# Low parts of eleven mixer weight tiles: an adding transfer onto negative high parts in place of VectorE's subtraction

## The chip, the cores and the metric

One core of one Trainium2 chip runs the whole program. The metric is device microseconds of one execution; lower is better. All tensors that cross the boundary are 32-bit floats.

## The reference, cut to what matters

The program is two transformer blocks, each of depth 2, over 512 tokens of width 1024. The change touches the second block alone, in its mixer stage, which runs once per layer (so twice):

```python
for l in range(DEPTH):                       # DEPTH = 2
    h = rmsnorm_2(x, norm_mix_g[l]) * (1.0 + sc1) + sh1
    u = h @ w_in[l]                          # 1024 -> 20 tiles of 128 columns, and 4 forget columns
    fq, fk, fv, ff, pu, rq, rk, rv, rg, cu = jnp.split(u, bounds, axis=-1)
    y_fox  = fox_attention(fq, fk, fv, ff, fox_fb[l])
    y_pool = pool_mixer(pu, pool_w[l], pool_scale[l])
    y_ret  = retention(rq, rk, rv, rg, positions, ret_gn_g[l])
    y_conv = conformer_conv(cu, conv_w[l], conv_b[l], conv_ln_g[l], conv_ln_b[l])
    mix = jnp.concatenate([y_fox, y_pool, y_ret, y_conv], axis=-1)
    x = x + g1 * (mix @ w_out[l])
    ...                                      # then the feed-forward stage
```

`conformer_conv` contains a causal convolution of 31 taps per channel over 256 channels.

## The kernel before, in words

TensorE multiplies in a fast 32-bit format (fp32r) that keeps fewer bits than a float. To keep the precision, every operand `x` is held as two tiles: a high part `hi` (the value rounded to fp32r, written by ScalarE, ACT) and a low part `lo = x - hi` (written by VectorE, DVE). A product is then three matmuls, `hi*hi`, `hi*lo` and `lo*hi` (`mm3`, lines 289 to 291: two with the weight's high part and one with its low part).

Weights are streamed. `weight_plan` (line 338) lists every weight tile in the order of use; for the mixers these are, per layer, twenty tiles of `w_in2` of 1024 x 128 values (on the chip 128 partitions x 1024 values, 512 KB), numbered t = 0 to 19, with the small tile `w_ff` ahead of t = 11, and then eight tiles of `w_out2`. Four of the twenty (`QB2`: 5, 8, 11 and 14) are scaled by 0.125 while they are split. Three steps bring a tile in:

- `load` (line 106) issues the transfer from HBM into a raw tile `wraw` on SyncE's queue (SP, line 118). There are four raw buffers; a load waits until the last reader of the tile four places back is done.
- `cut_tile` (line 184) splits it. It takes a pair `whi`, `wlo` from a pool with **two** buffers each, so the pair of tile t can only be written when TensorE has finished tile t - 2. ACT writes `whi` (line 203, or 206 for the scaled tiles), and DVE writes `wlo` (line 204, or 207).
- `next` (line 217) hands the pair to a product; it splits two tiles ahead.

In the mixers, `Mix.dense` (line 1689) multiplies one weight tile with the 512 tokens: 8 times `mm3` into a PSUM tile `dps`, of which there are two. What evacuates `dps` depends on the tile: t = 0 to 3 feed the convolution's gate, t = 4 to 6, 7 to 9, 11 to 13 and 14 to 16 are the query, key and value of four head pairs (for the first two pairs with a rotation, `roped`, lines 1767 to 1772), t = 10 and 17 feed the pooling mixer, 18 and 19 a gate.

Beside that runs the convolution, on DVE alone: `taps` (lines 2094 to 2103) issues 31 multiply-adds of 128 x 512 values for each of two channel halves, spread over the steps of the products. The scheduler is told to place each of them behind the latest weight split (`K.W.last`, lines 214 and 2098). Between the products stand the retention's and the forgetting attention's matmuls (lines 1956, 1987, 1837 and others).

The order of each engine's queue is settled when the program is built: a scheduler orders the instructions of each engine by its own model of their lengths, and on the chip every queue runs in that order. POOL (GpSimd) has little to do in the mixers: a few clears of small buffers (lines 274, 2045, 1830 and 2106) and some sums.

Of the kernel before, what the change touches and what calls it, by code (L numbers as in the profile page):

```python
# [13 lines left out]
AF = mybir.ActivationFunctionType  # L14
OP = mybir.AluOpType
# [36 lines left out]
QB1 = (9, 13, 17, 21, 26, 28, 31, 33)  # L52
QB2 = (5, 8, 11, 14)


def parts(x, bits):

    out = []
    for _ in range(3):
        e = math.floor(math.log2(abs(x)))  # L60
        c = math.floor(x / 2.0 ** (e - bits + 1)) * 2.0 ** (e - bits + 1)
        out.append(c)
        x -= c
    return out + [x]
# [6 lines left out]
def fr(ap):  # L71
    return ap.bitcast(F32)


class Weights:
# [5 lines left out]
    def __init__(self, K, raw, split, plan, bufs):  # L81
        self.K, self.tc, self.nc, self.raw, self.split, self.bufs = K, K.tc, K.nc, raw, split, bufs
        self.loads, self.cuts, self.sums = [], [], []
        for e in plan:
            n = len(self.loads)
            if e[0] == "S":
                self.loads += [(x, e[2] * 256) for x in e[1]]
                at = len(self.cuts)
                self.sums += [(at + i, f, n + m, e[2]) for i, f, m in
                              ((-4, self.sums12, 0), (-2, self.sums12, 2), (-1, self.sums34, 0), (0, self.sums34, 2))]  # L90
                self.cuts += [("S", i, n, e[2]) for i in range(7)]
            else:
                self.loads.append((e[0], e[1] * e[2]))
                self.cuts.append(("T", n, e[1], e[2], (e + (None,))[3]))
        self.tiles, self.freed, self.ready, self.by_pool = {}, set(), [], set()
        self.slots = {False: [], True: []}
        self.n_load = self.n_split = self.n_ring = 0
        self.st = {}
        self.extra = self.xraw = None
        self.depth = 2  # L100
# [80 lines left out]
                self.cut_tile(self.n_split, *c[1:])  # L181
            self.n_split += 1

    def cut_tile(self, at, n, kc, m, scale):
        self.load(n + 1)
        t = self.tiles[n]
        hi, lo = self.parts()
        if scale is None:
            pool = at in self.by_pool
            E = self.nc.gpsimd if pool else self.nc.vector  # L190
            step = kc * m // (PCH if pool else 1)
            if m < 64:

                w, hl = t[:, :kc * m].rearrange("p (k m) -> p k m", m=m), hi[:, :2 * kc * m]
                hl = hl.rearrange("p (k m) -> p k m", m=2 * m)
                self.nc.scalar.activation(hl[:, :, :m], w, AF.Copy)
                self.nc.vector.tensor_tensor(hl[:, :, m:], w, fr(hl[:, :, :m]), op=OP.subtract)
                self.ready.append((at, hl, None))
                self.free(n)
                return  # L200
            for o in range(0, kc * m, step):
                q = slice(o, o + step)
                s = self.nc.scalar.activation(hi[:, q], t[:, q], AF.Copy)  # L203
                v = E.tensor_tensor(lo[:, q], t[:, q], fr(hi[:, q]), op=OP.subtract)  # L204
        else:
            s = self.nc.scalar.activation(hi[:, :kc * m], t[:, :kc * m], AF.Copy, scale=scale)
            v = self.nc.vector.scalar_tensor_tensor(lo[:, :kc * m], t[:, :kc * m], scale, fr(hi[:, :kc * m]),
                                                op0=OP.mult, op1=OP.subtract)
        self.ready.append((at, hi[:, :kc * m].rearrange("p (k m) -> p k m", m=m),
                           lo[:, :kc * m].rearrange("p (k m) -> p k m", m=m)))  # L210
        if v.ins.engine == mybir.EngineType.DVE:
            self.last = s.ins, v.ins
        self.free(n)
# [68 lines left out]
class Kern:  # L282
# [54 lines left out]
    def weight_plan(self):  # L337
        a = self.a
        plan = []
        for l in range(2):  # L340
            for t in range(36):
                plan.append((a["w_in"][l, t], 8, 128, 0.125 if t in QB1 else None))
            for t in range(8):
                for p in range(2):
                    plan.append((a["w_out"][l, t, p], 6, 128))
        for l in range(2):
            for t in range(20):
                if t == 11:
                    plan.append((a["w_ff"][l], 8, 4))
                plan.append((a["w_in2"][l, t], 8, 128, 0.125 if t in QB2 else None))  # L350
            for t in range(8):
                plan.append((a["w_out2"][l, t], 8, 128))
            for f0, f1 in FGROUPS:
                f = f0
                while f < f1:
                    if f < FPLAIN:
                        plan += [(a["ffn_w1"][l, f], 8, 128), (a["ffn_w3"][l, f], 8, 128)]
                        f += 1
                    else:
                        plan.append(("S", [a[w][l, f + i] for w in ("ffn_w1", "ffn_w3") for i in range(2)], 4))  # L360
                        f += 2
                for t in range(8):
                    plan.append((a["ffn_w2"][l, t][:, f0 * 128:f1 * 128], f1 - f0, 128))
        return plan
# [2050 lines left out]
```

## Time and profile before

| | |
|---|---|
| three runs, us | 2479.31, 2479.59, 2483.43 (median 2479.59) |
| the profiled execution, us | 2483.87 |
| its span on the engines, us | 2482.1 |
| TensorE busy, share of the span | 95% |
| VectorE busy | 77% |
| ScalarE busy | 53% |
| GpSimd busy | 5% |
| mean granted clock of TensorE | 0.983 |

The profiled execution is 4.3 us above the median of the runs; 1.8 us of it lie outside the span. Matmuls are pipelined, so their busy times overlap: an idle TensorE is read from the gaps ahead of matmuls, not from the busy share. The products with the mixers' input weights run from 1286 to about 1440 us of the span in the first layer, and from 1892 to about 2050 us in the second.

### The profile page before, as it was taken

To read this page: it belongs to the slowest core of one execution; us is meant where nothing else is said; L and a number is where in the kernel's file an instruction comes from. 1 tells how busy PE (TensorE), PEld (TensorE's weight loads), DVE (VectorE), ACT (ScalarE), POOL (GpSimd) and SP (SyncE) were. 2 spreads that over 40 slices of the span, in tenths; PEclk is the share of its full clock that TensorE was granted. 3 is DMA by queue.
4 is the path that set the end of the run, shared out by engine and by line. 5 is a ranking of instruction groups with operands and counts; after the bars stand their busy time and mean duration, and the time that the engine had idled before them with its cause. 6 is when DMAs were issued, how large, how long until landed. Compare 5 with 4: busy or idle time off the path is not lost. (4 is left out here: it accounts for less than half of the span.)

```text
span 2482.1 us, 37640 instructions
## 1 busy us (share of the span) xinstructions
PE 2354.0 (95%) x14392; PEld 2028.6 (82%) x14392; DVE 1902.7 (77%) x3337; ACT 1326.0 (53%) x2595; POOL 113.0 (5%) x138
## 2 busy tenths in 40 slices
PE   7899999999999999999998899999999799999998
PEld 3788888888887788888786678989898578899997
DVE  5778777888457888798669868989767985967674
ACT  3566555667345665568644455535354455545453
POOL 0100000000011100000010101000001010100000
PEclk9999999999999999999999999999999999999999
DMA  6112333223422136641432122675432212242422
GB/s 257 51 50 92 96 105 100 85 88 100 153 81 76 45 124 204 211 131 50 135 99 67 58 63 86 215 242 208 141 102 74 69 57 68 85 137 69 136 65 72
DMA packets 87749, 269.67 MB, mean 109 GB/s; under 512 B 12049, under 2 KB 22545, under 8 KB 87185
## 3 DMA queue, kind: packets, MB, share of 16 engines
q1 hardware_dynamic: 78240, 232.79, 29.1%
q10 hardware_dynamic: 6912, 25.17, 2.9%
q0 software_dynamic: 2416, 9.31, 1.0%
q8 instruction: 113, 1.85, 0.3%
q14 instruction: 68, 0.55, 0.1%
HBM read 255.82 MB, written 11.40 MB: 108 GB/s over the span
## 5 line engine op out<-in xcount | busy, mean ns | idle before, releaser
L289 PE MATMUL dps<-hx,whi 128*128 128x512 f32 (+1 forms) x1040 | 412.7, 398 | 22.1 <-ACT q L1744 8.1
L291 PE MATMUL dps<-hx,wlo 128*128 128x512 f32 (+1 forms) x1040 | 400.1, 386 | 8.3 <-DVE wlo L204 4.3
L290 PE MATMUL dps<-hx,whi 128*128 128x512 f32 (+1 forms) x1040 | 401.0, 387 | 5.7 <-DVE hx L523 4.4
L203 ACT ACTIVATE whi<-wraw 128x1024 fp32r<-128x1024 f32 (+2 forms) x202 | 194.1, 964 | 272.6 <-issue 93.6
L204 DVE TENSOR_TENSOR wlo<-wraw,whi 128x1024 fp32r<-128x1024 f32 (+1 forms) x182 | 209.3, 1151 | 75.9 <-ACT whi L203 74.5
L289 PEld LDWEIGHTS dps<-hx,whi 128*128 128x128 f32 x1040 | 200.9, 193 | 51.3 <-ACT q L1744 8.9
L291 PEld LDWEIGHTS dps<-hx,wlo 128*128 128x128 f32 x1040 | 200.2, 193 | 44.5 <-DVE wlo L204 5.2
L290 PEld LDWEIGHTS dps<-hx,whi 128*128 128x128 f32 x1040 | 200.5, 193 | 31.5 <-DVE hx L523 7.1
L1162 ACT ACTIVATE ph<-PT 128x512 fp32r<-128x512 f32 (+1 forms) x280 | 152.8, 559 | 136.1 <-PE PT L1157 132.8
L1163 DVE TENSOR_TENSOR pl<-PT,ph 128x512 fp32r<-128x512 f32 (+1 forms) x280 | 175.2, 641 | 43.4 <-ACT ph L1162 41.2
L161 ACT ACTIVATE whi<-wraw 128x512 fp32r<-128x512 f32 x200 | 118.7, 625 | 102.5 <-PE spt L1520 38.4
L1145 PE MATMUL Y<-ph,vt 128*128 128x256 f32 (+1 forms) x592 | 161.8, 283 | 6.7 <-ACT ph L1162 2.8
L1157 PE MATMUL PT<-ident,P 128*128 128x128 f32 x1024 | 160.5, 276 | 5.8 <-DVE pl L1163 4.0
L1146 PE MATMUL Y<-pl,vt 128*128 128x256 f32 (+1 forms) x592 | 163.1, 291 | 2.4 <-DVE pl L1163 2.2
L290 PE MATMUL w2p<-g,whi 128*128 128x512 f32 (+1 forms) x364 | 140.9, 387 | 1.0 <-DVE g L299 1.0
L289 PE MATMUL w2p<-g,whi 128*128 128x512 f32 (+1 forms) x364 | 140.8, 387 | 0.0
L291 PE MATMUL w2p<-g,wlo 128*128 128x512 f32 (+1 forms) x364 | 140.6, 387 | 0.0
L1157 PEld LDWEIGHTS PT<-ident,P 128*128 128x128 f32 x1024 | 119.0, 141 | 23.1 <-DVE pl L1163 9.8
L1145 PEld LDWEIGHTS Y<-ph,vt 128*128 128x128 f32 x592 | 112.2, 190 | 28.5 <-ACT ph L1162 19.5
L1096 PE MATMUL S<-kt,qt 128*128 128x256 f32 (+2 forms) x576 | 127.3, 329 | 1.6 <-DVE nm L1114 0.9
L1146 PEld LDWEIGHTS Y<-pl,vt 128*128 128x128 f32 x592 | 112.3, 190 | 13.5 <-DVE pl L1163 6.0
L1115 ACT ACTIVATE P<-P,nm 128x512 f32<-128x512 f32 (+1 forms) x128 | 94.9, 742 | 47.7 <-DVE nm L1114 46.1
(474 smaller groups left out, 6387.6 us busy)
## 6 DMA issues: line engine op xcount, KB each, us to landing
wraw<-ffn_w SPq DMA_DIRECT2D x120, 512.0 KB, 4.4
wraw<-w_in SPq DMA_DIRECT2D x112, 512.0 KB, 3.5
adaw<-ada_wt SPq DMA_DIRECT2D x80, 512.0 KB, 4.0
adab<-ada_wt ACTq DMA_DIRECT2D x48, 512.0 KB, 5.1
wraw<-w_out SPq DMA_DIRECT2D x32, 384.0 KB, 3.1
aw<-ada_w SPq DMA_DIRECT2D x16, 512.0 KB, 10.2
wraw<-w_out SPq DMA_DIRECT2D x16, 512.0 KB, 3.5
bias<-bias_b SPq DMA_DIRECT2D x16, 384.0 KB, 3.7
```

The costliest lines, as they stand in the source:

```text
L161: self.nc.scalar.activation(hi[:, j * w:j * w + w], x, AF.Copy)
L203: s = self.nc.scalar.activation(hi[:, q], t[:, q], AF.Copy)
L204: v = E.tensor_tensor(lo[:, q], t[:, q], fr(hi[:, q]), op=OP.subtract)
L289: mm(ps, hi, xh, start=start, stop=False)
L290: mm(ps, hi, xl, start=False, stop=False)
L291: self.mm_last = mm(ps, lo, xh, start=False, stop=stop).ins
L1096: mm(S[:, so:so + n], Q[:, j, qc], Kt[:, i, ko:ko + n], start=i == 0, stop=i == 1)
L1145: mm(o, v, ph[:, co:co + w], start=b == 0 and n == 0, stop=False, skip_group_check=True)
L1146: mm(o, v, pl[:, co:co + w], start=False, stop=b == len(banks) - 1 and n == len(items) - 1, skip_group_check=True)
L1157: nc.tensor.transpose(pst[:, col:col + 128], ps[t][:, pc:pc + 128], K.ident)
L1162: A.activation(ph[:, :col], pst[:, :col], AF.Copy)
L1163: V.tensor_tensor(pl[:, :col], pst[:, :col], fr(ph[:, :col]), op=OP.subtract)
```

## The change

For eleven of the twenty tiles (t = 2, 3, 4, 6, 7, 9, 10, 12, 13, 15, 16), in both layers, the low part is made otherwise. ACT writes the negative of the rounded value into `wlo`; a transfer issued on POOL's queue then reads the same weight tile from HBM a second time and adds it onto `wlo` in place, which leaves `x - hi`; ACT writes `whi` as before. VectorE does nothing for these tiles. `K.W.last`, behind which the taps are placed, is not set by them.

```diff
+DMAT = (2, 3, 4, 6, 7, 9, 10, 12, 13, 15, 16)
...
-    def cut_tile(self, at, n, kc, m, scale):
+    def cut_tile(self, at, n, kc, m, scale, by_dma):
         self.load(n + 1)
         t = self.tiles[n]
         hi, lo = self.parts()
+        if by_dma:
+            w = kc * m
+            self.nc.scalar.activation(lo[:, :w], t[:, :w], AF.Copy, scale=-1.0)
+            self.nc.gpsimd.dma_start(lo[:, :w], self.loads[n][0], accum_op=OP.add)
+            self.nc.scalar.activation(hi[:, :w], t[:, :w], AF.Copy)
+            self.ready.append((at, *(x[:, :w].rearrange("p (k m) -> p k m", m=m) for x in (hi, lo))))
+            self.free(n)
+            return
         if scale is None:
...
-                plan.append((a["w_in2"][l, t], 8, 128, 0.125 if t in QB2 else None))
+                plan.append((a["w_in2"][l, t], 8, 128, 0.125 if t in QB2 else None, t in DMAT))
```

What the scheduler makes of it is seen in the queues. Lines of the changed kernel are 11 higher than those of the kernel before in everything below `cut_tile`.

ACT's queue at the start of the first layer's mixers, before (lines 203 and 206 write `whi`, 2086 evacuates a gate, 503 is part of a rotation, with half-tiles `t`):

```order
L203 ACTIVATE whi<-wraw 128x1024 x2
L2086 ACT_TABLE_LOAD
L2086 ACTIVATE th<-dps 128x512
L203 ACTIVATE whi<-wraw 128x1024
L2086 ACTIVATE th<-dps 128x512
L206 ACTIVATE whi<-wraw 128x1024
L203 ACTIVATE whi<-wraw 128x1024
L503 ACTIVATE t_13844<-dps 32x512 x3
```

The same stretch in the changed kernel (line 195 writes `whi`, 193 the negative into `wlo`, 217 a scaled `whi`):

```order
L195 ACTIVATE whi<-wraw 128x1024
L193 ACTIVATE wlo<-wraw 128x1024
L195 ACTIVATE whi<-wraw 128x1024
L2097 ACT_TABLE_LOAD
L2097 ACTIVATE th<-dps 128x512
L193 ACTIVATE wlo<-wraw 128x1024
L195 ACTIVATE whi<-wraw 128x1024
L2097 ACTIVATE th<-dps 128x512
L193 ACTIVATE wlo<-wraw 128x1024
L217 ACTIVATE whi<-wraw 128x1024
L195 ACTIVATE whi<-wraw 128x1024
L193 ACTIVATE wlo<-wraw 128x1024
```

The scheduler has put `whi` ahead of `wlo`, so the transfer of a tile starts two ACT instructions after its buffers come free, and for t = 3 and 4 a table load or an evacuation `th` stands between the two.

DVE's queue at the same place, before (204 and 207 are the subtractions, 2107 the gated input, 2100 and 2102 the taps):

```order
L204 TENSOR_TENSOR wlo<-wraw,whi 128x1024
L1842 CAST ck<-ones 64x512
L204 TENSOR_TENSOR wlo<-wraw,whi 128x1024
L2107 SCALAR_TENSOR_TENSOR hp_13599<-th,dps 128x512
L2100 TENSOR_SCALAR cacc_13601<-hp_13599,cw,v_13590 128x512
L2102 SCALAR_TENSOR_TENSOR cacc_13601<-hp_13599,cw,cacc_13601 128x512
L204 TENSOR_TENSOR wlo<-wraw,whi 128x1024
L2102 SCALAR_TENSOR_TENSOR cacc_13601<-hp_13599,cw,cacc_13601 128x512 x3
L2107 SCALAR_TENSOR_TENSOR hp_13600<-th,dps 128x512
L207 SCALAR_TENSOR_TENSOR wlo<-wraw,whi 128x1024
```

And in the changed kernel:

```order
L1853 CAST ck<-ones 64x512
L2118 SCALAR_TENSOR_TENSOR hp_13599<-th,dps 128x512
L2111 TENSOR_SCALAR cacc_13601<-hp_13599,cw,v_13590 128x512
L2113 SCALAR_TENSOR_TENSOR cacc_13601<-hp_13599,cw,cacc_13601 128x512 x4
L2118 SCALAR_TENSOR_TENSOR hp_13600<-th,dps 128x512
L218 SCALAR_TENSOR_TENSOR wlo<-wraw,whi 128x1024
```

The subtractions of t = 2, 3 and 4 are gone; the taps and the scaled tile's subtraction (t = 5) close up.

POOL's queue in the first layer's mixers, in the changed kernel (line 194 is the adding transfer; the kernel before has the same rows without it):

```order
L2117 MEMSET hp_13600 128x32
L194 DMA wlo<-w_in 128x1024 x7
L2056 MEMSET pb_14180 128x16
L2056 MEMSET pb_14181 128x16
L2056 MEMSET pb_14182 128x16
L194 DMA wlo<-w_in 128x1024 x2
L1841 MEMSET lf 128x512
L194 DMA wlo<-w_in 128x1024
L2142 TENSOR_TENSOR both<-cacc_13601,cacc_13602 128x512
L2025 TENSOR_TENSOR rst<-rst,nhalf 128x8
L194 DMA wlo<-w_in 128x1024
```

The eleven transfers stand in the order of the tiles; seven of them have nothing else of POOL's between them.

## Rows read from the trace of the kernel before

**Rows 1.** The page's first part: busy time, share of the span, instructions.
```profile
PE 2354.0 (95%) x14392; PEld 2028.6 (82%) x14392; DVE 1902.7 (77%) x3337; ACT 1326.0 (53%) x2595; POOL 113.0 (5%) x138
```

**Rows 2.** Busy time by stretch of the mixers: length, engines, granted clock, DMA share, GB/s.
```profile
1286.00:1304.00 18.00, 18.00 (x82) 14.61 (x81) 13.27 (x19) 6.38 (x7) 0.00 (x0) 1.00 0.42 140
1304.00:1346.00 42.00, 37.83 (x160) 29.48 (x159) 40.19 (x59) 21.74 (x35) 0.34 (x3) 0.96 0.17 51
1346.00:1398.00 52.00, 41.84 (x189) 30.20 (x187) 48.05 (x99) 20.43 (x34) 3.07 (x3) 0.97 0.24 78
1952.00:2004.00 52.00, 42.37 (x177) 31.06 (x175) 47.51 (x98) 20.37 (x35) 1.61 (x2) 0.90 0.24 77
```

**Rows 3.** Whom TensorE waited for, 1284 to 1412 us: total us, times, longest.
```profile
PE dps L289 <- ACT q L1744: 4.1, 2, 3.8
PE dps L289 <- DVE t L1767: 3.4, 2, 2.8
PE dps L291 <- DVE wlo L207: 2.0, 1, 2.0
PE yr L1987 <- ACT ph L298: 1.5, 1, 1.5
PE pm L289 <- ACT ph L298: 1.2, 1, 1.2
PE dps L289 <- ACT ft L1785: 0.8, 1, 0.8
...
PE cumps L1837 <- DVE lf L1832: 0.5, 1, 0.5
PE tps L1757 <- DVE ret L1993: 0.4, 1, 0.4
```

**Rows 4.** The same view in the second layer, 1890 to 2020 us.
```profile
PE dps L289 <- DVE t L1767: 3.1, 2, 2.8
```

**Rows 5.** DVE's groups by form, 1286 to 1398 us: count, busy, mean ns, idle before.
```profile
L2102 DVE SCALAR_TENSOR_TENSOR cacc<-hp,cw,cacc 128x512 f32<-128x512 f32 x60 | 43.4, 746 | 0.3
L204 DVE TENSOR_TENSOR wlo<-wraw,whi 128x1024 fp32r<-128x1024 f32 x10 | 12.2, 1215 | 2.4 <-ACT whi L203 2.4
```

**Rows 6.** ACT's timeline, 1283 to 1298 us: start, length, instruction, idle before and releaser.
```profile
1283.83 1.06 ACT L203 ACTIVATE whi<-wraw 128x1024 fp32r<-128x1024 f32 x1 [0.65 <-POOL ql L274]
1286.55 1.06 ACT L203 ACTIVATE whi<-wraw 128x1024 fp32r<-128x1024 f32 x1 [1.66 <-PE dps L290]
1287.63 1.28 ACT L2086 ACT_TABLE_LOAD   x1
1288.92 0.60 ACT L2086 ACTIVATE th<-dps 128x512 f32<-128x512 f32 x1
1291.97 1.06 ACT L203 ACTIVATE whi<-wraw 128x1024 fp32r<-128x1024 f32 x1 [2.45 <-PE dps L290]
1297.57 1.06 ACT L206 ACTIVATE whi<-wraw 128x1024 fp32r<-128x1024 f32 x1 [4.05 <-PE dps L290]
```

**Rows 7.** TensorE's timeline: the first matmuls of tile t = 2.
```profile
1286.41 0.39 PE L289 MATMUL dps<-hx,whi 128*128 128x512 f32 x1
1286.64 0.40 PE L290 MATMUL dps<-hx,whi 128*128 128x512 f32 x1
```

**Rows 8.** DMA issues: count, KB each, median us from issue to landing.
```profile
wraw<-w_in SPq DMA_DIRECT2D x112, 512.0 KB, 3.5
us<-T POOLq DMA_DIRECT2D x11, 384.0 KB, 2.6
x<-xt SPq DMA_DIRECT2D x1, 2048.0 KB, 8.2
```

**Rows 9.** POOL's transfers of line 1212: their instruction, ns min/median/max, first and last start.
```profile
L1212 POOL DMA_DIRECT2D us<-T x22: 539/542/731, 137.9 to 1179.7; - x22
```

**Rows 10.** Stretches right behind TensorE's two longest gaps; columns as in rows 2.
```profile
1332.00:1336.00 4.00, 4.00 (x12) 3.15 (x11) 3.91 (x7) 2.73 (x5) 0.14 (x2) 0.57 0.00 0
1376.00:1380.00 4.00, 2.92 (x6) 1.57 (x7) 3.97 (x12) 0.56 (x1) 0.00 (x0) 0.62 0.36 131
```

More of the change, by code (lines that the diff above doesn't have):

```diff
@@ L93, in __init__ @@
                 self.loads.append((e[0], e[1] * e[2]))
-                self.cuts.append(("T", n, e[1], e[2], (e + (None,))[3]))
+                self.cuts.append(("T", n, e[1], e[2], *(e[3:] + (None, False)[len(e) - 3:])))
         self.tiles, self.freed, self.ready, self.by_pool = {}, set(), [], set()
```

## The prediction

> **What bounds the kernel now.** I read the shares first, then the mixers by stretch, then TensorE's waits there. Over the span TensorE is busy for 95% [rows 1]; that is a mean over stages, and the change lives in two stretches of some 115 us. The view by stretch [rows 2] splits them. From 1286 to 1304 us TensorE has no gap (18.00 of 18.00) and DVE is busy for 13.27. From 1304 to 1346 it is the other way round: DVE is busy for 40.19 of 42, TensorE for 37.83. From 1346 to 1398 DVE has 48.05 of 52, TensorE 41.84. The second layer repeats this (42.37 and 47.51). So the first tiles are bound by TensorE and everything up to the end of the convolution's taps by DVE.
>
> The waits [rows 3] say what that costs. The lines shown sum to 13.9 us, four smaller ones left out. Nearly all lead back to DVE: a PSUM tile that the rotation has not yet emptied (3.4), a low part that comes late (2.0), and evacuations in which ACT and DVE take turns (4.1, 1.5, 1.2). The second layer's list is within 0.6 us of this one [rows 4].
>
> A gap has a second price. After the gaps of 2.8 and 3.8 us the granted clock of 4 us is 0.57 and 0.62 [rows 10], that is mostly the lower of the two levels (1.2 GHz), so about 4 x 0.43 = 1.7 us of full-speed work is lost behind each. After the wait of 2.0 us no such stretch shows in the first layer.
>
> **What is removed.** Eleven subtractions per layer; ten of them are in rows 5 with 1.215 us each, so 11 x 1.215 = 13.4 us of DVE per layer. In the stretches where DVE leads that takes its 88.24 of 94 us [rows 2] to about 79, and the taps (60 of them, 43.4 us [rows 5]) run earlier because nothing stands between them. I take it that the waits on DVE's backlog go: of the 4.1 all but 0.7, the whole of 3.4, 2.0, 0.5 and 0.4, and half of 1.5, 1.2 and 0.8 [rows 3]. That is 11.4; since such chains never close fully I count 11.0. With the two long gaps their clock losses go, 3.4. Removed per layer: **14.4 us**. This is DVE's whole saving seen on TensorE's path, a generous reading; the third rival takes a mean one.
>
> **What is added.** (a) ACT: eleven more passes of 1.06 us [rows 6], 11.7 us per layer on an engine that is busy for 48.55 of 112 us there [rows 2]. They lengthen evacuations that stand behind them; 1 us per layer. (b) POOL: eleven issues; one takes 0.54 us [rows 9] on an engine with 3.4 us of work in 112 [rows 2]. Behind a waiting transfer stand only clears of small buffers, a sum and a power, wanted later: nothing. Their cover is POOL's idleness; without it each would cost its 0.54. (c) SP: raw tiles are released after two ACT passes (2.12 us) instead of one and a subtraction (2.28): nothing. (d) The **new wait**: TensorE now waits for a transfer where it waited for DVE.
>
> The price of (d) hangs on one length that the trace does not show, L, from the issue of the adding transfer to TensorE's release. The nearest rows [rows 8]: a plain load of this size lands in 3.5 us; a load of 2048 KB in 8.2, so each further 512 KB costs (8.2 - 3.5) / 3 = 1.57 us; a store of 384 KB from POOL's queue lands in 2.6, so that queue by itself is not slower. Below 3.5 I see no reason for L to fall. An adding transfer must read its destination too: 3.5 + 1.57 = 5.1. And the raw tile's release starts the next raw load at the same moment: another 0 to 1.57. So 5.1 to 6.6, and I take the middle, **5.9**; the ends for the range are 3.5 and 8.2 (2048 KB: both reads, the write and the raw load, all in line).
>
> The Trainium skill, "Collectives: The Full Stack", section on the bandwidth ceiling, says that an add inside a transfer costs no cycles of its own but needs two source reads on one ring, which halves its rate; "DMA: Bandwidth & Descriptors", section on issuing engines, says that transfers of different issuing engines share the same 16 engines. By the first alone L would be 5.1 and the sum below minus 9 us; by both, 6.6 and plus 6. No row before shows an adding transfer.
>
> Now the tiles. TensorE needs 5.6 us for one (1291.97 to 1297.57, each the release of a buffer [rows 6]) and 0.23 per matmul [rows 7].
> - t = 2: `whi` starts at 1283.83, `wlo` is written by 1285.95 [rows 6]; TensorE starts the tile at 1286.41 [rows 7] and has four matmuls without a low part, to 1287.33. It waits L - 1.4.
> - t = 4: the buffers come free at the end of t = 2; then 1.06 + 0.60 + 1.06 = 2.7 [rows 6] and L, against one tile and two matmuls, 6.06. It waits L - 3.3.
> - t = 6: the same without the 0.60: L - 3.9. t = 9: four transposes on TensorE lie between: about L - 4.6.
> - t = 3, 7, 10: the second of two neighbours starts its chain while the first waits; the first's wait covers it. Nothing.
> - t = 12, 13, 15, 16: attention matmuls lie between the tiles (TensorE 41.84 of 52 [rows 2]); nothing at 5.9, something above 7.
>
> Sum of the waits: 4L - 13.2, at 5.9 **10.4 us** per layer. Those of t = 2 (4.5) and t = 4 (2.6) are near or above the gaps that lost the clock: 3.4.
>
> **The sum.** Per layer 10.4 + 3.4 + 1.0 - 14.4 = +0.4 us, for two layers about +1. Against the profiled execution 2483.87 that gives 2485; it stands 4.3 us above the median, so the median becomes **2481**: no change, out of two large terms that cancel. Runs of this kernel can tell 0.2%, 5 us, from nothing.
>
> **The rivals.**
> 1. *The adding transfer is little longer than a load*, L = 3.5 to 5.1. At 3.5 only t = 2 waits (2.1, under the gaps that cost the clock) and t = 4 (0.2): 2.3 + 1 - 14.4 = -11 per layer, -22. At 5.1: 7.2 + 1.7 + 1 - 14.4 = -4.5, -9. In the middle 2464. For it: POOL's short stores [rows 8]. Against: the second read.
> 2. *TensorE's wait on the transfer becomes the bound of the dense tiles* (slower). L = 8.2: four waits of 19.6, four clock losses of 1.7, 1 of ACT: 27.4 - 14.4 = +13 per layer, +26, so 2506. It turns slower by over 0.2% at L = 6.4. For it: three streams of 512 KB meet (DMA share 0.42 already from 1286 to 1304 [rows 2]). Against: that share falls to 0.17 to 0.24 afterwards.
> 3. *DVE's relief does not reach TensorE*: only the waits named for DVE go (3.4 + 2.0) and one clock loss, 7.1; the turns of ACT and DVE stay, ACT being fuller. At 5.9: 14.8 - 7.1 = +7.7 per layer, +15, so 2495.
>
> **How the numbers follow.** The forecast, L from 5.1 to 6.6, gives 2471 to 2486 (-9 to +6): chance 0.42, of which 0.12 lie beyond 0.2% on the fast side, 0.20 within, 0.10 on the slow side. Rival 1: 0.26. Rival 2: 0.20. Rival 3: 0.12. Faster 0.12 + 0.26 = 0.38, same 0.20, slower 0.10 + 0.20 + 0.12 = 0.42. The range reaches from the fast end of rival 1, short of its last microseconds, to just past rival 2: 2460 to 2508.
>
> **What would show it.** The transfers of line 194 landing in 5 to 6.6 us. TensorE's waits in 1286 to 1346 us: a line `dps L302 <- DMA wlo` with about four waits, the first near 4.5 us; the waits on `t` (line 1778 there) and on the scaled `wlo` gone. DVE busy for some 79 of those 94 us. Granted clock below 1 right after t = 2, where it is 1.00 now. The forecast is wrong if the waits on the transfer sum to under 5 or over 16 us per layer, or if TensorE's waits on ACT and DVE stay above 8.

## The result and the profile after

The changed kernel takes 2510.19 us (median of 6 runs, 2505.11 to 2513.12) against 2481.11 for the kernel before, run beside it (6 runs, 2479.31 to 2483.68). The ratio is 1.0116, with a 95% interval of 1.0100 to 1.0132: slower by 29 us. The forecast was 2481 with a range that ended at 2508, so the time lies just outside, on the slow side. The profiled execution has a span of 2508.6 us.

The page shows where the work went. TensorE has the same 14392 matmuls and is busy for 10 us more than in [rows 1], because some of them ran at a lower clock; VectorE (DVE) has 22 instructions fewer, ScalarE (ACT) 22 more. The second fence holds the queue of the adding transfers and their issues.

```profile
PE 2363.9 (94%) x14392; PEld 2034.8 (81%) x14392; DVE 1879.1 (75%) x3315; ACT 1345.9 (54%) x2617; POOL 131.9 (5%) x160
```

The same page's parts on DMA: queue, kind, packets, MB, share of 16 engines; then the issues, with KB each and median us to landing.

```profile
q0 software_dynamic: 5584, 20.84, 3.5%
...
wlo<-w_in POOLq DMA_DIRECT2D x22, 512.0 KB, 6.7
```

The answer for line 194, the transfer itself, gives the spread of that length:

```profile
L194 POOL DMA_DIRECT2D wlo<-w_in x22: 842/855/935, 1284.5 to 2035.6; - x22
...
DMA to landing us min/median/max: 5.3/6.7/8.0
```

Whom TensorE waited for in the first layer's mixers, 1284 to 1425 us (total, times, longest). Line numbers after the change are 11 higher than in [rows 3]:

```profile
PE dps L302 <- DMA wlo<-w_in: 16.9, 5, 5.3
PE dps L300 <- ACT q L1755: 4.1, 1, 4.1
PE yr L1998 <- ACT ph L309: 1.5, 1, 1.5
PE dps L300 <- ACT whi L195: 0.6, 1, 0.6
PE cumps L1848 <- DVE lf L1843: 0.5, 1, 0.5
PE tps L1768 <- ACT ft L1796: 0.2, 1, 0.2
```

Set this beside [rows 3]. The waits on `t` (3.4), on the scaled `wlo` (2.0), on `pm` (1.2) and most of that on `ft` (0.8) are gone. In their place stands one line of 16.9 us. The waits on `q` and `yr`, which the prediction had mostly or half removed, stand there unchanged.

TensorE's timeline has the five gaps one by one; they are the first low-part matmuls of tiles t = 2, 4, 6, 9 and 12. The sixth row is the old wait on `q`. (Some expectations below put the fifth gap before tile 13. TensorE runs the 24 matmuls of tile 11 and two more right ahead of it, and the eighth transfer, which is tile 12's, ends it: it was issued at 1368.09 and landed after 8.0 us.)

```profile
1291.97 0.80 PE L302 MATMUL dps<-hx,wlo 128*128 128x512 f32 x1 [5.25 <-DMA wlo<-w_in]
...
1308.14 0.50 PE L302 MATMUL dps<-hx,wlo 128*128 128x512 f32 x1 [3.40 <-DMA wlo<-w_in]
...
1323.33 0.80 PE L302 MATMUL dps<-hx,wlo 128*128 128x512 f32 x1 [2.19 <-DMA wlo<-w_in]
...
1346.18 0.50 PE L302 MATMUL dps<-hx,wlo 128*128 128x512 f32 x1 [2.87 <-DMA wlo<-w_in]
...
1376.15 0.50 PE L302 MATMUL dps<-hx,wlo 128*128 128x512 f32 x1 [3.17 <-DMA wlo<-w_in]
...
1391.18 0.56 PE L300 MATMUL dps<-hx,whi 128*128 128x512 f32 x1 [4.10 <-ACT q L1755]
```

Each gap has its second price. The view by stretch (columns as in [rows 2]) shows the granted clock in the 4 us behind each of the five gaps, and in the 8 us behind the wait on `q`. The first row is the whole piece of the program from the mixers' first memset to the convolution's first statistics, 442 matmuls, which the rest of this document uses to compare kernels.

```profile
1280.43:1411.21 130.78, 106.31 (x442) 80.73 (x443) 95.16 (x173) 59.29 (x87) 14.61 (x22) 0.91 0.47 109
...
1292.00:1296.00 4.00, 4.00 (x10) 3.16 (x11) 0.35 (x1) 0.00 (x0) 0.00 (x0) 0.51 0.81 176
1308.00:1312.00 4.00, 3.86 (x12) 3.05 (x13) 2.88 (x5) 0.00 (x0) 0.00 (x0) 0.69 0.40 128
1323.00:1327.00 4.00, 3.67 (x9) 2.92 (x10) 3.25 (x6) 3.70 (x7) 0.67 (x1) 0.57 0.73 105
1346.00:1350.00 4.00, 3.82 (x11) 3.10 (x12) 3.47 (x6) 2.88 (x5) 0.11 (x1) 0.64 0.94 210
1376.00:1380.00 4.00, 3.85 (x18) 2.97 (x19) 1.57 (x5) 2.27 (x4) 0.85 (x1) 1.00 0.29 46
1391.00:1395.00 4.00, 3.27 (x5) 1.47 (x6) 3.94 (x10) 0.72 (x2) 0.00 (x0) 0.56 0.00 0
1395.00:1399.00 4.00, 4.00 (x12) 2.98 (x11) 3.61 (x7) 1.61 (x3) 0.00 (x0) 0.59 0.63 151
```

The same piece of the program in the kernel before, for comparison:

```profile
1282.11:1396.81 114.70, 99.90 (x442) 76.33 (x442) 105.39 (x182) 50.44 (x78) 4.43 (x12) 0.97 0.25 80
```

So the piece became 16.1 us longer per layer. Of that, idle time of TensorE is (130.78 - 106.31) - (114.70 - 99.90) = 9.7 us, and 106.31 - 99.90 = 6.4 us are the same 442 matmuls at a lower clock. The clock rows account for the second part: behind four of the new gaps 4 us x (0.49 + 0.31 + 0.43 + 0.36) = 6.4 us are lost, and behind the wait on `q` 4 us x (0.44 + 0.41) = 3.4, together 9.8, where the kernel before lost 4 us x (0.43 + 0.38) = 3.2 behind its two long gaps [rows 10]; the difference is 6.6. In the second layer the same piece grew by 15.4 us (115.64 to 131.08). Together that is 32 us, and 29 were measured.

### The profile page after: what moved, and what is told of

Same layout as the page of the kernel before. It is cut to its first block, busy times and chain, and to the rows that moved or that the text cites. A ratio compares the mean times of both kernels' runs of the same rounds, so it can differ in the third digit from the quotient of the medians.

```text
span 2508.6 us, 37687 instructions
## 1 busy us (share of the span) xinstructions
PE 2363.9 (94%) x14392; PEld 2034.8 (81%) x14392; DVE 1879.1 (75%) x3315; ACT 1345.9 (54%) x2617; POOL 131.9 (5%) x160
## 5 line engine op out<-in xcount | busy, mean ns | idle before, releaser
L302 PE MATMUL dps<-hx,wlo 128*128 128x512 f32 (+1 forms) x1040 | 406.0, 392 | 37.7 <-DMA wlo<-w_in 33.1
L300 PE MATMUL dps<-hx,whi 128*128 128x512 f32 (+1 forms) x1040 | 417.4, 402 | 15.1 <-ACT q L1755 8.2
L301 PE MATMUL dps<-hx,whi 128*128 128x512 f32 (+1 forms) x1040 | 406.1, 392 | 6.0 <-DVE hx L534 4.9
L214 ACT ACTIVATE whi<-wraw 128x1024 fp32r<-128x1024 f32 (+2 forms) x180 | 170.7, 952 | 219.2 <-issue 81.6
L300 PEld LDWEIGHTS dps<-hx,whi 128*128 128x128 f32 x1040 | 204.2, 197 | 43.3 <-ACT q L1755 8.6
L215 DVE TENSOR_TENSOR wlo<-wraw,whi 128x1024 fp32r<-128x1024 f32 (+1 forms) x160 | 182.6, 1142 | 68.0 <-ACT whi L214 66.7
L301 PEld LDWEIGHTS dps<-hx,whi 128*128 128x128 f32 x1040 | 203.9, 197 | 33.0 <-DVE hx L534 7.7
L1157 PEld LDWEIGHTS Y<-pl,vt 128*128 128x128 f32 x592 | 111.8, 189 | 13.7 <-DVE pl L1174 6.3
## 6 DMA issues: line engine op xcount, KB each, us to landing
aw<-ada_w SPq DMA_DIRECT2D x16, 512.0 KB, 10.2
```

What stands on the lines that cost most here:

```text
L300: mm(ps, hi, xh, start=start, stop=False)
L301: mm(ps, hi, xl, start=False, stop=False)
L302: self.mm_last = mm(ps, lo, xh, start=False, stop=stop).ins
L1157: mm(o, v, pl[:, co:co + w], start=False, stop=b == len(banks) - 1 and n == len(items) - 1, skip_group_check=True)
```

## The experiments

**Theory A**: TensorE waits for a chain (ScalarE's pass, then a transfer of 6.7 us), this wait and the clock behind it are the loss, and VectorE's relief is real but much smaller than was forecast. **Theory B**, the rival: ScalarE's eleven extra passes delay the evacuations. Further rivals on the length of the transfer are named where they are tested. All runs were timed beside the kernel before; the last column is (ratio - 1) x 2480 us with its interval.

| kernel | median us | ratio (95%) | us against before |
|---|---|---|---|
| changed kernel | 2510.2 | 1.0116 (1.0100 to 1.0132) | +29 (25 to 33) |
| negative pass first | 2499.8 | 1.0085 (1.0060 to 1.0111) | +21 (15 to 28) |
| copy instead of add | 2477.6 | 0.9998 (0.9985 to 1.0011) | 0 (-4 to 3) |
| no transfer | 2465.1 | 0.9951 (0.9937 to 0.9964) | -12 (-16 to -9) |
| low-part matmuls last | 2476.9 | 0.9996 (0.9983 to 1.0008) | -1 (-4 to 2) |
| before, low-part matmuls last | 2482.8 | 1.0010 (0.9998 to 1.0022) | +2 (0 to 5) |
| late four tiles only | 2474.3 | 0.9979 (0.9969 to 0.9988) | -5 (-8 to -3) |
| early seven tiles only | 2507.1 | 1.0112 (1.0090 to 1.0134) | +28 (22 to 33) |
| hidden version | 2464.6 | 0.9934 (0.9919 to 0.9949) | -16 (-20 to -13) |
| hidden version, faster taps | 2468.1 | 0.9951 (0.9937 to 0.9964) | -12 (-16 to -9) |
| zero low parts | 2462.0 | 0.9932 (0.9912 to 0.9953) | -17 (-22 to -12) |
| source in SBUF | 2477.8 | 0.9997 (0.9985 to 1.0009) | -1 (-4 to 2) |
| third buffer, cut earlier | 2500.9 | 1.0080 (1.0057 to 1.0104) | +20 (14 to 26) |
| raw tile held | 2499.2 | 1.0081 (1.0066 to 1.0096) | +20 (16 to 24) |
| high part as source | 2503.3 | 1.0100 (1.0075 to 1.0124) | +25 (19 to 31) |
| hidden version, source in SBUF | 2464.1 | 0.9939 (0.9922 to 0.9957) | -15 (-19 to -11) |

### The transfer taken out

```diff
-            self.nc.gpsimd.dma_start(lo[:, :w], self.loads[n][0], accum_op=OP.add)
```

> The transfer is taken out and everything else stays: the low part of the eleven tiles is the negative high part that ScalarE writes, so the addition of the raw weights is left out. It shows what VectorE's relief and ScalarE's extra passes are worth without the transfer. The prediction's terms (14.4 us removed, 1.0 us of ScalarE added per layer) give 2481 - 27 = 2454 us or less. Theory A (of TensorE's waits only those on t, on the scaled low part and some small ones go, 8.7 us per layer and one clock loss of 1.7, because the taps keep their pace and the 4.1 us wait on ScalarE's q stays) gives 2458 to 2466 us. Theory B (ScalarE's passes eat the relief) gives 2478 us or more.

Measured: 2465 us, 12 under the kernel before. This splits the change in two. Everything but the transfer (VectorE relieved, ScalarE with eleven more passes) is worth -12 us, not the -27 of the prediction's terms; it lies in theory A's bracket. The transfer alone costs the rest, (1.0116 - 0.9951) x 2480 = 41 us, not the prediction's 28.

TensorE's waits in the same piece of the program say what went. Line numbers are one lower than in the changed kernel.

```profile
PE dps L299 <- ACT q L1754: 4.1, 1, 4.1
PE dps L299 <- DVE t L1777: 1.7, 2, 1.3
PE yr L1997 <- ACT ph L308: 1.5, 1, 1.5
...
PE cumps L1847 <- DVE lf L1842: 0.3, 1, 0.3
PE dps L301 <- DVE wlo L217: 0.3, 1, 0.3
PE tps L1767 <- ACT ft L1795: 0.2, 1, 0.2
```

Against [rows 3]: `t` 3.4 became 1.7, the scaled `wlo` 2.0 became 0.3, `pm` and `ft` are off the list. `q` and `yr` kept all they had. The view by stretch for this kernel's same 442 matmuls:

```profile
1280.27:1387.86 107.59, 99.00 (x443) 76.59 (x443) 94.74 (x173) 59.42 (x87) 6.01 (x12) 0.97 0.28 85
```

It is 7.1 us shorter than before: 6.2 of idle time and 0.9 of busy time. VectorE shed 105.39 - 94.74 = 10.7 us in it, so two thirds reached TensorE. In the second layer the piece is 9.2 us shorter (115.64 to 106.47), of which 3.7 are busy time, since TensorE's clock there rises from 0.94 to 0.97. One place where relief was lost shows in whom VectorE itself waited for in the first 24 us, 1280 to 1304:

```profile
DVE hp L2117 <- ACT th L2096: 4.1, 1, 4.1
DVE hp L2117 <- PE dps L301: 3.9, 1, 3.9
```

The subtractions of the first tiles are gone, and VectorE stands idle for 8.0 us instead (2.1 us on these two waits in the kernel before): the next instruction in its queue is the convolution's input `hp`, which needs ScalarE's gate and a PSUM tile that TensorE has not finished. No tap moved into that time.

### The negative pass first

```diff
-            self.nc.scalar.activation(lo[:, :w], t[:, :w], AF.Copy, scale=-1.0)
+            s = self.nc.scalar.activation(lo[:, :w], t[:, :w], AF.Copy, scale=-1.0)
...
-            self.nc.scalar.activation(hi[:, :w], t[:, :w], AF.Copy)
+            with self.tc.issue_after(s.ins):
+                self.nc.scalar.activation(hi[:, :w], t[:, :w], AF.Copy)
```

> The pass that writes the negative high part goes first on ScalarE and the plain high part second, so each transfer starts one ScalarE pass (1.06 us) earlier; nothing else changes. Theory A (TensorE waits for the chain ScalarE pass, then transfer of 6.7 us, and this is the loss): each of the five waits per layer on the transfer (5.3, 3.4, 2.2, 2.9, 3.2 us) is about 1.0 us shorter, some 5 us of idle time per layer and a little of the clock loss, so 2494 to 2500 us. Theory B (the loss is ScalarE's eleven extra passes, which delay the evacuations): the same passes are there, so 2508 to 2512 us, the changed kernel's own time.

Measured: 2499.8, at the slow end of theory A's bracket. The five waits became four of 5.3, 2.6, 2.2 and 1.4 us, 11.4 in all against 16.9. The first tile gained nothing. This speaks against theory B, which has the same passes here: moving one pass by a microsecond moved the time by 0.3%. But the intervals of the two kernels just overlap, so the next section has to decide.

### Low-part matmuls last, and its control

```diff
-                K.mm3(ps, hi[:, k, :], lo[:, k, :], B.h[0][:, k, :], B.h[1][:, k, :], k == 0, k == 7)
+                for j in range(3 * k, 3 * k + 3):
+                    w, x, c = (hi, B.h[j % 2], j // 2) if j < 16 else (lo, B.h[0], j - 16)
+                    K.mm_last = self.nc.tensor.matmul(ps, w[:, c, :], x[:, c, :], start=j == 0, stop=j == 23).ins
```

> The changed kernel with the 24 matmuls of a dense tile in another order: the 16 with the high part first, then the 8 with the low part, in the same PSUM tile. The first low part is wanted after 16 matmuls (3.7 us) instead of two (0.5 us). Theory A: the waits on the transfer shrink by up to 3.3 us each: 5.3 to about 2, 3.4 to about 0, the others to 0, some 13 us of idle time per layer and most of the clock loss of 6 us behind them, so 2472 to 2484 us. Theory B (ScalarE): 2505 us or more.

> A control for the reordered matmuls: the kernel before the change (VectorE subtracts) with the 16 high-part matmuls of each dense tile first and the 8 low-part ones last. Theory A: this order is worth only the waits on the low part that are there, 2.0 us per layer and perhaps a clock loss: 2472 to 2480 us; then the 33 us that the same order gave the changed kernel are the hidden transfer. Rival: the order itself makes TensorE faster, and gives the kernel before 20 to 33 us as well: 2446 to 2460 us.

Measured: the same reorder takes the changed kernel from 2510 to 2477 and the kernel before from 2481.5 to 2482.8. The gain is therefore the hidden transfer and not the order itself, and theory B (2505 us or more) is out. TensorE's waits in the changed kernel with this order, first two lines of the list (the matmuls now stand on line 1711):

```profile
PE dps L1711 <- DMA wlo<-w_in: 5.6, 2, 3.6
PE dps L1711 <- ACT q L1757: 4.0, 1, 4.0
```

16.9 us in five waits became 5.6 in two, while the transfers landed in 6.8 us, no sooner than before. The larger, 3.6 us, is tile 2; the other, 2.0, is tile 7, whose negative pass stands behind evacuations in ScalarE's queue. In the control the wait of 2.0 us on the scaled low part went, and a wait of 2.8 us on the convolution's sum came up later, which theory A had not foreseen.

### Copy instead of add

```diff
-            self.nc.gpsimd.dma_start(lo[:, :w], self.loads[n][0], accum_op=OP.add)
+            self.nc.gpsimd.dma_start(lo[:, :w], self.loads[n][0])
```

> The transfer stays, with its bytes, its queue and its waits, but copies instead of adding: the addition of the negative high part is left out. Theory C (the add's second read is the price): it lands in 3.5 to 5.1 us against 6.7, the four dense waits shrink by 4 x 1.6 to 4 x 3.2 us per layer, and the time is 2480 to 2497 us. Rival D (the length is that of POOL's queue for a transfer of this size, add or no add): it lands in 6 us or more and the time is 2503 to 2512 us.

Measured: 2477.6 with a landing of 4.6 us: theory C, a little faster than its range. The program has every instruction of the changed kernel in the same order; only the add is off. Queue and landing in 1280 to 1425 us (queue, packets, MB, share of 16 engines), and then, from the answer for line 194, us to landing over the whole run:

```profile
q0 software_dynamic: 1584, 5.77, 11.4%
```

```profile
DMA to landing us min/median/max: 3.7/4.6/6.7
```

The changed kernel in the same stretch:

```profile
q0 software_dynamic: 1584, 5.77, 21.9%
```

The same packets and bytes take 21.9 / 11.4 = 1.9 times the engine time when they add. The Trainium skill, "Collectives: The Full Stack", section on the bandwidth ceiling, says of a reduce-scatter that its add is slow not for the arithmetic but because it needs two source reads on one ring; this pair of rows agrees with it on engine time. On the landing the ratio is smaller, 6.7 / 4.6 = 1.5.

### Which tiles: the late four, the early seven

```diff
-DMAT = (2, 3, 4, 6, 7, 9, 10, 12, 13, 15, 16)
+DMAT = (12, 13, 15, 16)
```

> Only tiles 12, 13, 15 and 16, which lie among attention matmuls, get the transfer; the dense tiles 2 to 10 keep VectorE's subtraction. Theory A (the loss arises in the dense tiles, and the late ones cost the 3.2 us wait before tile 13 with its clock loss, less what VectorE's backlog gives back): 2478 to 2490 us. Theory P, the prediction's (late transfers are covered, and four subtractions fewer where VectorE is busy for 48 of 52 us reach TensorE): 2467 to 2475 us.

> The other half of the split: tiles 2 to 10 with the transfer, 12 to 16 with VectorE's subtraction. The late four alone gave -7 us. Theory A, the parts add up (the loss is all in the dense tiles): 2510 + 7 = 2517, from 2510 to 2522 us. Rival I (in the changed kernel the late four cost the wait of 3.2 us before tile 13 and the clock behind it, because the early ones have put the program out of step): without them 2496 to 2506 us.

(The second has `DMAT = (2, 3, 4, 6, 7, 9, 10)`.) Measured: the late four alone give -5 us, the early seven alone +28. The first contradicts theory A's expectation and bears out the prediction's: by themselves the late transfers are covered, and about half of the relief arrives (eight subtractions of 1.215 us are 9.7). TensorE's waits, 1284 to 1425 us, of the kernel with the late four, first four lines of the list:

```profile
PE dps L300 <- ACT q L1755: 4.1, 1, 4.1
PE dps L300 <- DVE t L1778: 3.4, 2, 2.8
PE dps L302 <- DVE wlo L218: 2.0, 1, 2.0
PE yr L1998 <- ACT ph L309: 1.5, 1, 1.5
```

No wait on a transfer is in the whole list. Tile 12 shows why. Here its transfer is issued at 1349.00 us, lands after 6.4 and is wanted only at 1358.62, in part because tile 11's low part, from VectorE, is 2.0 us late. In the changed kernel it is issued at 1368.09, wanted at 1372.97 and lands after 8.0, beside two weight loads and one of the pooling weights issued from 1367.12 to 1368.20. The early seven gave 2507 us, between the two expectations; their intervals (22 to 33) and that of the changed kernel (25 to 33) overlap, so what the late four do when the early ones are there too can't be told from nothing.

### ScalarE's passes

```diff
-            self.nc.scalar.activation(lo[:, :w], t[:, :w], AF.Copy, scale=-1.0)
-            self.nc.gpsimd.dma_start(lo[:, :w], self.loads[n][0], accum_op=OP.add)
```

with one tile of zeros in the place of `lo`.

> Neither VectorE nor ScalarE nor a transfer makes the low part of the eleven tiles: their low-part matmuls read one tile of zeros, so the low parts are left out of the result. Against the kernel without the transfer (2465 us) it takes away ScalarE's eleven extra passes alone. The prediction counts 1 us per layer for them: 2461 to 2465 us. Rival: VectorE's relief is worth the 14.4 us that the prediction removed, and the passes eat half of it: 2448 to 2457 us.

Measured: 2462 us, inside the prediction's bracket. The intervals of this kernel and of the one without the transfer overlap (0.9912 to 0.9953, 0.9937 to 0.9964), so the passes cost between nothing and some 11 us in all, 3 by the medians; the prediction had 2. The rival, a relief of 14.4 us per layer half eaten by ScalarE, is out: with no pass and no transfer the whole relief is 17 us for two layers.

### What sets the transfer's length

```diff
-            self.nc.gpsimd.dma_start(lo[:, :w], self.loads[n][0], accum_op=OP.add)
+            self.nc.gpsimd.dma_start(lo[:, :w], t[:, :w], accum_op=OP.add)
```

> The adding transfer takes the raw weights from the tile in SBUF, where the plain load has put them, instead of reading them from HBM a second time. Theory C (the price is the add's work in the DMA engines, wherever its source lies): it lands in 6 to 7.5 us as now, and the time is 2505 to 2520 us (the raw tile is also held until the transfer is over). Rival H (the second read of HBM beside the raw load is the price): it lands in 5.5 us or less and the time is 2485 to 2498 us.

Measured: 2477.8. By the landing rival H seemed to hold, though the time is under its range. Line 194's landing in this kernel, and its queue in 1280 to 1425 us:

```profile
DMA to landing us min/median/max: 4.5/4.6/7.4
```

```profile
q0 software_dynamic: 1584, 5.77, 20.9%
```

The engine time is still doubled, yet the transfer lands 2.1 us sooner. But this edit changes two things. The raw tile is also held until the transfer has landed: in the changed kernel the next raw load is issued at 1284.40 us and the transfer at 1284.46; here the transfer is issued at 1284.98 and the raw load at 1290.04. Two more kernels take the two apart.

```diff
             self.nc.gpsimd.dma_start(lo[:, :w], self.loads[n][0], accum_op=OP.add)
...
+            self.nc.gpsimd.tensor_tensor(self.dum, t[:, :1], fr(lo[:, :1]), op=OP.add)
```

> The transfer reads HBM as in the changed kernel, but the raw tile is released only when it has landed (an operation of one column on POOL reads both), so the next raw load starts behind it and not beside it. Theory N (the raw load beside it is the price of the long transfer): it lands in 4.5 to 5.2 us, TensorE's waits on it sum to 5 to 9 us per layer, and the time is 2474 to 2486 us. Theory H (the price is an add whose source is HBM): it lands in 6 us or more and the time is 2500 to 2515 us.

```diff
+            self.nc.scalar.activation(hi[:, :w], t[:, :w], AF.Copy)
             self.nc.scalar.activation(lo[:, :w], t[:, :w], AF.Copy, scale=-1.0)
-            self.nc.gpsimd.dma_start(lo[:, :w], self.loads[n][0], accum_op=OP.add)
-            self.nc.scalar.activation(hi[:, :w], t[:, :w], AF.Copy)
+            self.nc.gpsimd.dma_start(lo[:, :w], fr(hi[:, :w]), accum_op=OP.add)
```

> The transfer adds the high part (an SBUF tile) instead of the raw weights, so the low part comes out as zero and is left out of the result; the raw tile is released as in the changed kernel, and the next raw load runs beside the transfer. Every engine has the instructions of the changed kernel in the same order. Theory N: it lands in 6 us or more and the time is 2498 to 2512 us. Theory H: it lands in 4.5 to 5.2 us and the time is 2474 to 2486 us.

Landing with the raw tile held, then (second fence) with the high part as source:

```profile
DMA to landing us min/median/max: 5.3/5.6/7.1
```

```profile
DMA to landing us min/median/max: 4.5/6.2/9.7
```

| median us to landing | raw load beside it | raw load behind it |
|---|---|---|
| source in HBM | 6.7 | 5.6 |
| source in SBUF | 6.2 | 4.6 |

Neither theory holds alone. The raw load beside the transfer costs 1.1 to 1.6 us, the source in HBM 0.5 to 1.0. The kernel with the raw tile held shows the first within itself: in its first layer the transfers of tiles 7 and 10, issued 0.2 and 0.3 us behind a raw load after all, land in 6.9 and 6.5 us, and the five with no other transfer beside them in 5.3 to 5.6. The Trainium skill, "DMA: Bandwidth & Descriptors", section on issuing engines, says that transfers of all issuing engines share the same 16 engines; the columns of this table agree.

In the changed kernel's time these lengths do what the prediction's formula says: the four waits of the dense tiles should sum to 4L - 13.2. With the high part as source (6.2) that is 11.6, and the trace has 4.9 + 3.2 + 2.3 + 2.3 = 12.7; with the raw tile held (5.6) 9.2, and 3.9 + 2.5 + 1.4 + 1.6 = 9.5; with the raw tile as source (4.6) 5.2, and 2.8 + 1.3 + 0.7 + 0.6 = 5.4. With the copy the median (4.6) gives 5.2, and the trace has 4.5 + 1.6 + 0.7 + 0.7 = 7.5: tile 2's copy alone took 6.7, and with each tile's own landing (6.7, 4.5, 4.6, 4.6) the formula gives 7.2. The kernel with the raw tile held missed its time (2499 instead of 2474 to 2486) for its length and for a wait that the formula has at nothing. Tile 7, elsewhere covered by tile 6's wait, waits 1.6 us: tile 6's transfer lands sooner, and tile 7's own takes 6.9, with the raw load that tile 6's landing let go (issued at 1320.71) beside it. The seven waits sum to 12.4.

### Another cure: more buffers

```diff
...
+            if self.n3 % 3 == 0:
+                return [pool.tile([128, KD * 128], F32R, tag="whi", name="whi"),
+                        self.lo3.tile([128, KD * 128], F32R, tag="wlo3", bufs=1, name="wlo")]
...
-            self.cut(at + (n or self.depth))
+            self.cut(at + (n or (3 if self.lo3 is not None else self.depth)))
```

and the negative pass first.

> Another cure than the order of the matmuls: a third buffer for the low parts in the mixers, tiles cut one further ahead, and the negative pass first on ScalarE, so that a transfer starts while the tile before last still runs. Theory A (the chain is bound by the release of the two buffers): the wait before tile 2 stays (5 us), those before 4, 6 and 9 go (8.5 us per layer) with most of their clock loss: 2480 to 2492 us. Rival: ScalarE's queue or the transfers' own rate holds the chain, and it is no better than the negative pass first alone, 2497 to 2503 us.

Measured: 2500.9, the rival's number, but not for its reason. Of the waits on the transfer only the one before t = 2 (4.2 us) is left in the first layer, and in the second one of 0.8, as theory A says. But TensorE's waits on `q` and `t`, from 1284 to 1425 us, are 5.4 and 3.8 us there (4.1 and none in the changed kernel). And a wait of another kind appeared where the second layer's mixers begin:

```profile
1890.10 0.58 PE L309 MATMUL dps<-hx,wlo 128*128 128x256 f32 x1 [10.24 <-DMA fb<-fox_fb]
```

The releaser named is a 2 KB load that has nothing to do with this tile. POOL's timeline shows what does: it subtracts tile 1's low part (two halves of 1.2 us), and this now starts at 1888.79, behind the tile 2 that was cut ahead and a memset that waits 8.8 us for the modulation. Without the stall of 10.2 us the time would be some 2484 to 2491, an estimate (10.2 less than the profiled execution's 2494.6 or the median); that kernel was not run. With the deeper cut in the path of POOL's own work, the buffers are an unsettled cure.

### A version that beats both

```diff
-DMAT = (2, 3, 4, 6, 7, 9, 10, 12, 13, 15, 16)
+DMAT = (3, 4, 6, 7, 9, 10, 12, 13, 15, 16)
```

with the low-part matmuls last and the negative pass first, as above. Two variants follow: in the first, `TRATE = (3, 3)` becomes `(2, 2)`; in the second, the transfer's source is `t[:, :w]`.

> The changed kernel with everything that the waits point to: high-part matmuls first and low-part ones last, the negative pass first on ScalarE, and tile 2, whose chain can't begin early, back with VectorE, which idles there. Theory A: the two waits on the transfer that are left with the new order (3.6 and 2.0 us per layer) go to about 0 and 1, with their clock loss: some 8 us per layer less than the new order alone, 2459 to 2466 us, at or under the kernel that has no transfer at all (2465). Theory B (the transfers' traffic or ScalarE's passes cost something beyond the waits): 2470 us or more.

> The same as the hidden version, but the taps of the convolution are handed to VectorE at every second step of the program instead of every third. Theory A says that VectorE's relief is lost because the taps keep their pace: with the faster pace they end earlier, fewer stand ahead of the evacuations before the wait on q (4.1 us), and the time falls under the hidden version's, to 2446 to 2460 us. Rival: VectorE is then too full in the dense tiles, TensorE waits for t again, and the time is 2466 to 2480 us.

> The raw tile in SBUF as the source, the low-part matmuls last, the negative pass first, tile 2 with VectorE. If the transfer costs nothing but its wait, the last wait on it (0.8 us per layer) goes and the time is that of the hidden version or a little less, 2459 to 2465 us, which is also that of the kernels without a transfer (2462 to 2465). If its traffic or the held raw tile costs something, 2468 us or more.

Measured: 2464.6 us, 16 under the kernel before and 45 under the changed one. TensorE's waits, 1284 to 1425 us, first three lines, and behind them the same 442 matmuls by stretch:

```profile
PE dps L1712 <- ACT q L1758: 4.1, 1, 4.1
PE dps L1712 <- ACT whi L196: 0.8, 1, 0.8
PE dps L1712 <- DMA wlo<-w_in: 0.8, 1, 0.8
```

```profile
1278.59:1386.89 108.30, 99.30 (x442) 76.30 (x443) 95.92 (x174) 58.59 (x86) 13.76 (x21) 0.97 0.53 127
```

The transfers run as long as ever (median 6.7 us) and the DMA share is 0.53, yet the stretch is within 0.7 us of that without any transfer (107.59) and the clock is back at 0.97. With the source in SBUF too (landing 4.5) the time is the same, 2464.1. So no cost of the transfer beyond its wait shows; the hidden version with its transfer taken out, which would settle that, was not run.

The faster taps gained nothing (2468.1, which can't be told from 2464.6: the intervals overlap). Their waits are worth reading (1284 to 1425 us, first four lines), though the profiled execution, 2476 us, is the slowest of its eight:

```profile
PE dps L1712 <- ACT ft L1799: 4.9, 2, 3.0
PE dps L1712 <- DVE t L1781: 3.6, 1, 3.6
PE pm L301 <- ACT ph L310: 1.8, 1, 1.8
PE dps L1712 <- ACT q L1758: 1.4, 1, 1.4
```

Half of theory A is borne out: the wait on `q`, which stands at 3.8 us or more in every other version of the changed kernel, falls from 4.1 to 1.4 us with the faster taps. Half of the rival is too: in this execution the waits on `t` and `ft` (8.5 us) take more than was won.

## Why the prediction was wrong

**The price of the wait (d)** is the term that failed on the added side. Three things make up its 41 us against 28.

- *L was taken as 5.9 us; it is 6.7.* The formula was right: 4L - 13.2 = 13.6, and the four dense waits sum to 5.25 + 3.40 + 2.19 + 2.87 = 13.7; tile by tile it is off by up to 0.8. The prediction had the parts of L (a load, the second read, the raw load beside it) but priced the second read and the neighbour from the slope of a larger load, 1.57 each at most, and then took the middle. Measured, the add costs 2.1 us over a copy from the same queue, and the copy itself takes 4.6, not 3.5, in that place.
- *"t = 12, 13, 15, 16: attention matmuls lie between the tiles ... nothing at 5.9, something above 7."* Tile 12 waits 3.2 us in the first layer and 2.5 in the second. Between tiles 11 and 12 there is no attention matmul: the 26 matmuls ahead of the gap are tile 11's 24 and two of tile 12. Its transfer took 8.0 us, so the clause "above 7" held. The late tiles alone do not wait.
- *The clock.* 3.4 us was put behind two gaps; four gaps lost 6.4 us, and behind the wait on `q`, which was to go, the loss over 8 us grew from 1.7 (clock 0.62 and 0.96) to 3.4.

**The removed term, 14.4 us per layer**, is the step that failed on the other side. Without the transfer the change is worth 12 us for two layers where the terms gave 27. In the first layer nothing of the wait on `q` went (3.4 forecast), 1.7 of the 3.4 on `t`, and 0.9 us of busy time where 3.4 of clock loss was counted. A part of the reason stands in the step's own words, "the taps run earlier because nothing stands between them". VectorE's queue is in a fixed order in which a tap follows so many steps of TensorE's program; in the first 24 us VectorE now waits for 8.0 us on ScalarE's gate and on TensorE. And the wait on `q` (4.1, of which all but 0.7 was struck out) is a sequence of ScalarE and VectorE turns with taps between them; it is 3.8 us or more in every version of the changed kernel but that with faster taps. How much of the missing relief each of the two accounts for is not shown. The prediction saw in its first reading that the tiles up to 1304 us were bound by TensorE, and then priced the relief as if all eleven subtractions stood where VectorE leads.

**What was right**: the waits on `t` and on the scaled low part went, tile 2 waits longest and the clock falls right behind it, the waits on ACT and DVE fell below 8 us (6.9), ScalarE's passes are cheap (3 us by the medians), three of the four late tiles are covered. By the prediction's own signs it was wrong: the waits on the transfer sum to 16.9 us in the first layer, over its 16. It saw that wait and relief work against each other; the size was off, since both errors (15 us of relief, 13 of wait) went the same way.

**The rivals.** The second came closest in time (2506), but at a length of 8.2 that no median shows. The third (the relief does not reach TensorE, 7.1 per layer removed) comes near the first layer's measured 7.1 us, but in part by luck: it is made of other waits and a clock loss, the measured figure has ScalarE's passes already taken off, and the second layer has 9.2. The outcome is both at once: a relief nearer to that size than to 14.4, and a wait at 6.7. In the prediction's terms the two together give 13.6 + 3.4 + 1.0 - 7.1 = 10.9 us per layer, +22, and tile 12's wait makes most of the rest. They had been given chances as if only one could happen.

## What to carry to other kernels

Price relief by the stretch and by the queue: an instruction taken from a busy engine is worth something only where the next one in its queue is ready, and that one may be waiting for the very engine one hopes to speed up. A transfer put on the path is a latency and not a rate, so first look for work of the consumer that doesn't need it: here the same 24 matmuls in another order hid a transfer of 6.7 us and turned +29 us into -1, and with the chain started earlier and tile 2 back on VectorE into -16. And when two of several rivals don't exclude each other, work out the time of both together.

## What the runs showed that was not expected

- An adding transfer of 512 KB takes 1.9 times the engine time of a copy (21.9% against 11.4% of 16 engines in the same stretch), wherever its source lies (20.9% from SBUF), but its landing moves with source and neighbour, from 4.6 to 6.7 us.
- The length that TensorE's clock loses behind a gap does not follow from the gap alone: behind 2.2 us before t = 6 the granted clock was 0.57, behind 3.2 us before t = 12 it was 1.00, both in the changed kernel.
- POOL's instruction for an adding transfer takes 0.86 us (line 194), that for the copy of the same size 0.53, and the store in [rows 9] 0.54.
- A releaser can be misnamed: the stall of 10.2 us put down to a 2 KB load was POOL's late subtraction.
